# Position bias built behind the first feature-major chunk, and read back eight heads at a time

## The chip, the cores and the metric

The kernel runs on one core of one Trainium2 chip. Its engines are named as the profile names them: PE is TensorE (products, and PEld its weight loads), DVE is VectorE, ACT is ScalarE, POOL is GpSimd, SP is SyncE, whose queue issues the loads of weights. The metric is the device time of one execution in microseconds (us), as a median over runs.

## The reference

Two transformer blocks run one after the other on 256 tokens of width 1024, in float32. The change lies in the first block's mixer. It normalizes x, multiplies it by `w_in`, and runs two attentions on pieces of the product: `dsa_mixer` (8 heads, the 64 best keys of each query by an index score) and `nsa_mixer` (8 heads in 2 groups, three branches: compressed tokens, selected blocks, a window). All logits get a position bias that depends on the distance of query and key alone:

```python
bias = table_a[t5_bucket(dist)]                     # heads 0 to 7, dsa_mixer
bias_c = table_b[t5_bucket(t - cmp_end)]            # heads 8 to 15, compressed tokens
bias_s = tg[g_idx, t5_bucket(dist_s)]               # heads 8 to 15, selected blocks
bias_w = table_b[t5_bucket(dist_w)]                 # heads 8 to 15, window
...
blk = kv[:, idx] + pe[None, None, :, None, :]       # 15 overlapping blocks of 32 tokens
return jax.nn.gelu(blk @ w1) @ w2                   # compress_blocks, for k and for v
```

## The kernel before

Weights stream from HBM in units of 512 KB (two k-tiles of 512 columns). SP's queue loads a unit into `raw` (L246), ACT rounds it into `hi` (L262), DVE subtracts to get the remainder `lo` (L263), and PE multiplies the normalized, transposed x by both parts: a *streamed product* below is one such matmul (L349, L351, L352 where the output is feature-major, L305 to L307 where it is token-major). Units are loaded up to five ahead of their use and split up to two ahead.

The first block's projection is cut into nine chunks of columns, in the order 4, 0, 1, 3, 2, 5, 6, 7, 8 (48 streamed products for chunk 4, 72 for chunk 0, 96 for each of the others). Small work of other kinds is queued with `later` and put between the k-tiles of these chunks: the index scores and their top 64 (`index`, `topk`), the compression of keys and values (`cmp1`, `cmp1b`, `cmp2`), then the attention steps during chunks 5 to 8. On PE, DVE and ACT the order of instructions is a scheduler's, which follows the program's dependencies; on POOL and SP it is the order of the code, since `manual_schedule` is set for these two.

The position bias is made by `bias_job` (L588 to L602). A product of the one-hot buckets with the table `rel_bias` gives `tv`, 16 heads by 384 distances (L590, L592). It is written to DRAM sixteen times over (`tvd`, L595) and read back with a shifted start for each partition, in eight DMAs of 16 partitions and 256 KB each, so that `BT[p, h, j]` is the bias of query p and key j for head h (L597). Then `cmpB`, the bias of the compressed tokens with its mask, is set and filled by two copies out of BT (L600 to L602). `bias_job` is queued behind the top 64 and falls into chunk 3.

On POOL the following stands behind it in the code: memsets of `kcT` and `VB` (L741, L743), of `ge` for k and v in `cmp1b` (L773), and the gates (L988). Ahead of it stand the loads of the compression's weights `w1k`, `w1v` and small operands `csk`, `csv` (L703, L705), the copies of k and v into shifted pairs `kpk`, `kpv` (L717, L718) and the additions that make the blocks `blkk`, `blkv` (L725). Compression multiplies the blocks by `w1` (`cmp1`, L753), folds four partial sums (`cmp1b`, L763), applies the gelu on DVE and ACT into `ge` (L774) and multiplies by `w2` (`cmp2`, L783 for k, L790 for v). BT's readers are `cmpB`, the softmax of the branches (L866, heads 8 to 15) and `bm` on POOL (L842, heads 0 to 7 with the mask of the top 64). The branches come in the order selected, window, `dsa_mixer`, so that heads 0 to 7 are read last.

Of the kernel before, what the change touches and what calls it, by code (L numbers as in the profile page):

```python
# [23 lines left out]
NEG = -1.0e30  # L24
# [185 lines left out]
class Prog:  # L210
# [343 lines left out]
    def block1_mix(self, x0, x):  # L554
        tc, nc, ap, g = self.tc, self.nc, self.ap, self.g
        with ExitStack() as es, ExitStack() as rs_:
# [22 lines left out]
            tot = sum(CONSTS[n].shape[1] for n in C1)  # L579
            BT = cp.tile([128, 16, 256], F32, name="BT")  # L580
            cmpB = cp.tile([128, 2, 8, 16], F32, name="cmpB")
# [5 lines left out]

            def bias_job():  # L588
                ps = self.psm()
                nc.tensor.matmul(ps[:16, :384], rb, onehot, start=True, stop=True)  # L590
                tv = bp.tile([16, 384], F32, name="tv")
                nc.vector.tensor_tensor(tv, ps[:16, :384], neg, op=ALU.add)  # L592

                tvd = self.dp.tile([16, 16, 384], F32, name="tvd")
                nc.gpsimd.dma_start(tvd.rearrange("c h u -> h c u"), tv.unsqueeze(1).to_broadcast([16, 16, 384]))  # L595
                for i in range(8):
                    nc.gpsimd.dma_start(BT[16 * i:16 * i + 16, :, :],  # L597
                                        bass.AP(tensor=tvd.tensor, offset=tvd.offset + 127 - 16 * i,
                                                ap=[[16 * 384 - 1, 16], [384, 16], [1, 256]]))
                nc.gpsimd.memset(cmpB, NEG)  # L600
                nc.gpsimd.tensor_copy(cmpB[:, 1, :, 0:15], BT[:, 8:16, 31:256:16])
                nc.gpsimd.tensor_copy(cmpB[:, 0, :, 0:7], BT[:, 8:16, 159:256:16])  # L602

# [22 lines left out]
            def small_done(t, ps):  # L626
                nc.scalar.activation(tms[:, t, :], ps, AF.Copy, scale=r0[:, t:t + 1])
                if t:
                    nc.scalar.activation(gb, tms[:, :, 328:352], AF.Tanh, scale=0.5)
                    nc.gpsimd.tensor_scalar(gb, gb, 0.5, 0.5, op0=ALU.mult, op1=ALU.add)  # L630
                    nc.gpsimd.dma_start(caus, ap["c1"][:, tot - 256:])
                    nc.gpsimd.dma_start(rest, ap["c1"][0:32, 128:896])
                    nc.gpsimd.dma_start(rb, ap["rel_bias"])
            stats()
            self.gemm_tok(W_IN1, 4, *xT, small_done, acc=self.psm)
# [14 lines left out]
            self.later(rsB_job)  # L650
            self.gemm_feat(W_IN1, 0, *xT, d0)


# [47 lines left out]
            for nm in "kv":  # L701
                w1 = mp.tile([128, 16, 128], F32, name="w1" + nm)
                nc.gpsimd.dma_start(w1, ap["cmp_w1_" + nm])  # L703
                cs = mp.tile([128, 80], F32, name="cs" + nm)
                nc.gpsimd.dma_start(cs, ap["cmp_s_" + nm])  # L705
                cw.append((w1, cs))
            blks = []

            def d1(i, ps):
                nc.vector.tensor_tensor(kv[:, 2 * i:2 * i + 2, :], ps, bc2, op=ALU.mult)  # L710
                if i:
                    return
                for i, nm in enumerate("kv"):
# [6 lines left out]
                    blk = mp.tile([128, 16, 32], F32, name="blk" + nm)  # L720
                    nc.gpsimd.memset(blk[:, :, 30:32], 0.0)
                    for gr in range(2):
                        v = bass.AP(tensor=kp.tensor, offset=kp.offset + 256 * gr,
                                    ap=[list(kp.ap[0]), [2, 16], [16, 15]])
                        nc.gpsimd.tensor_tensor(blk[:, :, 15 * gr:15 * gr + 15], v,  # L725
                                                cw[i][1][:, 0:16].unsqueeze(2).to_broadcast([128, 16, 15]),
                                                op=ALU.add)
                    blks.append(blk)
            self.gemm_feat(W_IN1, 1, *xT, d1)

            def dq(q):
# [3 lines left out]
                return f  # L735
            self.later(bias_job)
            self.gemm_feat(W_IN1, 3, *xT, dq(qb))


            kcT = cp.tile([128, 2, 16], F32, name="kcT")  # L740
            nc.gpsimd.memset(kcT, 0.0)  # L741
            VB = cp.tile([128, 2, 4, 64], F32, name="VB")
            nc.gpsimd.memset(VB, 0.0)  # L743
            cps = {}
# [14 lines left out]
            def cmp1b(i):  # L759

                nm = "kv"[i]
                ps = self.psm()
                nc.tensor.matmul(ps[:, :32], cps[i], fold, start=True, stop=True)  # L763
                hx = mp.tile([128, 30], F32, name="hx" + nm)
                nc.vector.tensor_copy(hx, ps[:, :30])
                u = mp.tile([128, 30], F32, name="u" + nm)
                nc.vector.tensor_tensor(u, hx, hx, op=ALU.mult)
                nc.vector.tensor_scalar(u, u, 0.044715, 1.0, op0=ALU.mult, op1=ALU.add)
                nc.vector.tensor_tensor(u, u, hx, op=ALU.mult)
                th = mp.tile([128, 30], F32, name="th" + nm)  # L770
                nc.scalar.activation(th, u, AF.Tanh, scale=0.7978845608028654)
                ge = mp.tile([128, 2, 16], F32, name="ge" + nm)
                nc.gpsimd.memset(ge, 0.0)  # L773
# [50 lines left out]
            for br in (1, 2, 0):  # L824
                for t in (1, 0):
                    nh = 2 if t else 4
                    for u in range(4 // nh):
# [6 lines left out]
                        duos.append(duo)  # L834
            box = {}

            def bm(U):
# [3 lines left out]
                U["bm"] = bmp.tile([128, nh, n], F32, tag="bm", name="bm")  # L841
                nc.gpsimd.tensor_tensor(U["bm"], BT[:, h0:h0 + 2 * nh - 1:2, j0:j0 + n],  # L842
                                        M[:, t, :n].unsqueeze(1).to_broadcast([128, nh, n]), op=ALU.add)
# [15 lines left out]
            def softmax(U, ps):  # L859
# [4 lines left out]
                for i, h in enumerate(U["heads"]):  # L864
                    b = U["bm"][:, i, :] if br == 0 else BT[:, 8 + h, j0:j0 + n]
                    nc.vector.tensor_tensor_reduce(L[:, i, :], ps[:, i, :], b, op0=ALU.add, op1=ALU.max, scale=1.0,  # L866
# [769 lines left out]
```

## Time and profile before

| | |
|---|---|
| median of 3 runs | 1128.43 us (1125.5 to 1130.07) |
| profiled execution | 1129.25 us, of it span 1127.5 us |
| PE busy | 1104.7 us, 98% |
| DVE, ACT, POOL busy | 762.8, 573.7, 93.3 us |
| mean granted clock of PE | 0.993 |
| chain that ended last | PE 92%, DVE 3%, DMA 3%, of which BT<-tvd 2% of the span |

The profiled execution's time holds 1.75 us beside the span, which runs from the first to the last instruction. The chain that ended last is followed back from the end: 92% of it is work of PE. PE is busy in nearly all the span, so the places that matter are those at which it is not, and those at which its clock is lowered; both are found in time with the waits of PE and with windows.

### The profile page before, as it was taken

How to read it: one execution, taken by the hardware profiler on the slowest of the kernel's cores; microseconds unless marked ns; L12 is line 12 of the kernel's file. 1: busy time of each engine (PE TensorE's matmuls, PEld its weight loads, DVE VectorE, ACT ScalarE, POOL GpSimd, SP SyncE). 2: the span in 40 equal slices, each digit the busy share in tenths (PEclk: the TensorE clock that was granted, in tenths of full speed). 3: DMA queues.
4: the chain of work that ended last, by engine and by line, in shares of the span. 5: the costliest groups of instructions: out<-in, count | busy, mean ns of one | idle time of the engine just before them, and what ended most of it. 6: DMA issues, size and time to landing. Idle time of an engine off the chain costs nothing.

```text
span 1127.5 us, 17685 instructions
## 1 busy us (share of the span) xinstructions
PE 1104.7 (98%) x6852; PEld 986.4 (87%) x6852; DVE 762.8 (68%) x1230; ACT 573.7 (51%) x858; POOL 93.3 (8%) x135
## 2 busy tenths in 40 slices
PE   9998999999999999999999999999999999999997
PEld 8887899888888878888879999889999978888886
DVE  6766777677755567777458675556778777777643
ACT  6325544555544456555445336545555455655542
POOL 1411230000001010000001010001323000000000
PEclk9998999999999999999999999999999998999999
DMA  8794124655555646555556655444544565555552
GB/s 298 250 175 145 39 86 149 210 179 196 189 187 182 199 168 201 186 187 186 186 169 201 195 168 200 152 130 139 181 150 157 163 204 167 188 186 185 189 173 92
DMA packets 55908, 196.91 MB, mean 175 GB/s; under 512 B 6716, under 2 KB 6988, under 8 KB 55568
## 3 DMA queue, kind: packets, MB, share of 16 engines
q1 hardware_dynamic: 52704, 186.44, 50.2%
q0 software_dynamic: 2832, 9.21, 3.5%
q8 instruction: 54, 0.88, 0.3%
q14 instruction: 30, 0.25, 0.1%
q10 hardware_dynamic: 288, 0.14, 0.1%
HBM read 192.84 MB, written 1.44 MB: 172 GB/s over the span
## 4 chain that ended last, share of the span: by engine, by line
PE 92%; DVE 3%; DMA 3%; ACT 1%; issue 1%; POOL 0%; DVEq 0%; POOLq 0%; ACTq 0%
PE acc L368 20%; PE acc L369 10%; PE acc L305 10%; PE acc L306 9%; PE acc L307 9%; PE acc L351 8%; PE acc L349 8%; PE acc L352 8%; DMA BT<-tvd 2%; PE sm L854 2%; PE o L893 1%; DVE lo L263 1%; PE tr L880 1%; PE o L1437 1%; PE sm L1407 1%; PE tr L399 1%
## 5 line engine op out<-in xcount | busy, mean ns | idle before, releaser
L263 DVE TENSOR_TENSOR lo<-raw,hi 128x1024 fp32r<-128x1024 f32 (+2 forms) x356 | 433.3, 1219 | 264.8 <-ACT hi L262 262.4
L262 ACT ACTIVATE hi<-raw 128x1024 fp32r<-128x1024 f32 (+2 forms) x356 | 371.2, 1044 | 425.4 <-issue 120.9
L368 PE MATMUL acc<-xs,hi 128*128 128x512 f32 x960 | 340.4, 400 | 1.3 <-DVE sum L374 1.0
L369 PE MATMUL acc<-xs,lo 128*128 128x256 f32 x960 | 268.8, 281 | 0.0
L368 PEld LDWEIGHTS acc<-xs,hi 128*128 128x128 f32 x960 | 180.8, 189 | 44.8 <-DVE sum L374 1.4
L349 PE MATMUL acc<-xs,hi 128*128 128x256 f32 (+1 forms) x696 | 198.7, 288 | 0.3 <-ACT hi L262 0.3
L351 PE MATMUL acc<-xs,hi 128*128 128x256 f32 (+1 forms) x696 | 198.1, 286 | 0.0
L352 PE MATMUL acc<-xs,lo 128*128 128x256 f32 (+1 forms) x696 | 197.0, 286 | 0.1
L369 PEld LDWEIGHTS acc<-xs,lo 128*128 128x128 f32 x960 | 181.9, 189 | 0.5
L349 PEld LDWEIGHTS acc<-xs,hi 128*128 128x128 f32 (+1 forms) x696 | 132.9, 192 | 3.4 <-issue 2.4
L351 PEld LDWEIGHTS acc<-xs,hi 128*128 128x128 f32 (+1 forms) x696 | 133.5, 192 | 1.9 <-issue 1.5
L352 PEld LDWEIGHTS acc<-xs,lo 128*128 128x128 f32 (+1 forms) x696 | 132.8, 192 | 1.6 <-issue 1.0
L305 PE MATMUL acc<-hi,hT 128*128 128x512 f32 x304 | 117.9, 390 | 1.0 <-DVE x L1069 1.0
L306 PE MATMUL acc<-lo,hT 128*128 128x512 f32 x304 | 118.5, 390 | 0.0
L307 PE MATMUL acc<-hi,hT 128*128 128x512 f32 x304 | 118.0, 389 | 0.0
L305 PEld LDWEIGHTS acc<-hi,hT 128*128 128x128 f32 x304 | 57.1, 188 | 13.3 <-DVE x L1069 1.5
L307 PEld LDWEIGHTS acc<-hi,hT 128*128 128x128 f32 x304 | 57.1, 188 | 12.0
L306 PEld LDWEIGHTS acc<-lo,hT 128*128 128x128 f32 x304 | 57.1, 188 | 11.5
L305 PE MATMUL acc<-hi,xs 128*128 128x386 f32 (+1 forms) x128 | 47.7, 375 | 1.6 <-DVE f L1160 1.5
L306 PE MATMUL acc<-lo,xs 128*128 128x386 f32 (+1 forms) x128 | 48.0, 375 | 0.0
L307 PE MATMUL acc<-hi,xs 128*128 128x386 f32 (+1 forms) x128 | 46.8, 370 | 0.0
L374 DVE TENSOR_TENSOR sum<-acc,sum 128x512 f32<-128x512 f32 x60 | 41.0, 684 | 0.0
(430 smaller groups left out, 1344.5 us busy)
## 6 DMA issues: line engine op xcount, KB each, us to landing
raw<-in_w_in SPq DMA_DIRECT2D x100, 512.0 KB, 3.5
raw<-in_ffn_w_gate SPq DMA_DIRECT2D x44, 512.0 KB, 3.5
raw<-in_ffn_w_up SPq DMA_DIRECT2D x44, 512.0 KB, 3.4
raw<-in_ffn_w_down SPq DMA_DIRECT2D x44, 512.0 KB, 3.4
raw<-in_w_mlp_in SPq DMA_DIRECT2D x32, 512.0 KB, 3.4
raw<-in_w_mlp_out SPq DMA_DIRECT2D x32, 512.0 KB, 3.2
raw<-in_w_out SPq DMA_DIRECT2D x16, 512.0 KB, 3.5
raw<-in_w_in SPq DMA_DIRECT2D x16, 386.0 KB, 3.1
```

Of the source, the lines that this page charges most:

```text
L262: nc.scalar.activation(hi[:, :n * w], raw[:, :n * w], AF.Copy)
L263: nc.vector.tensor_tensor(lo[:, :n * w], raw[:, :n * w], hi[:, :n * w], op=ALU.subtract)
L305: nc.tensor.matmul(ps[t][:, :w], xh[:, k, sl], hi, start=(k == 0), stop=False)
L306: nc.tensor.matmul(ps[t][:, :w], xh[:, k, sl], lo, start=False, stop=False)
L307: self.last_mm = nc.tensor.matmul(ps[t][:, :w], xl[:, k, sl], hi, start=False, stop=last)
L349: nc.tensor.matmul(o, hi[:, fs], xh[:, k, :], start=(k == 0 and f % 2 == 0), stop=False, skip_group_check=True)
L351: nc.tensor.matmul(o, hi[:, fs], xl[:, k, :], start=False, stop=False, skip_group_check=True)
L352: nc.tensor.matmul(o, lo[:, fs], xh[:, k, :], start=False, stop=last, skip_group_check=True)
L368: nc.tensor.matmul(ps[:, f, :, :], hi[:, fs], x.both[:, k, :, :], start=(k == 0), stop=False)
L369: nc.tensor.matmul(ps[:, f, 0, :], lo[:, fs], x.hi[:, k, :], start=False, stop=last)
L374: nc.vector.tensor_tensor(s, ps[:, :, 0, :], s, op=ALU.add)
L854: nc.tensor.matmul(ps[:, i, :], q[pr:pr + 64, U["fts"][i], t * 128:t * 128 + 128], kk, start=True, stop=True)
```

## The change

The job is cut in two. `bias_table` makes `tv` and writes `tvd`; it is called right behind chunk 0 instead of being queued into chunk 3. `bias_rows(g)` reads back eight heads into a tile of their own: `BT[1]`, heads 8 to 15, ahead of chunk 1, and `BT[0]`, heads 0 to 7, behind the call of chunk 5. Each is eight DMAs of 16 partitions and 128 KB. The memsets of `kcT`, `VB`, `ge`, the tails of `blk` and `cmpB` are put ahead of the first read. The load of `w1k` and the small operands come behind that read, the copies kp of k and v come together, `w1v` behind them, then the additions and the two copies into `cmpB`. The operands `rest` and `rb` of the bias product are loaded ahead of the causal mask.

```diff
-            BT = cp.tile([128, 16, 256], F32, name="BT")
+            BT = [cp.tile([128, 8, 256], F32, name="BT%d" % g) for g in range(2)]
...
-            def bias_job():
+            box = {}
+
+            def bias_table():
+
                 ps = self.psm()
                 nc.tensor.matmul(ps[:16, :384], rb, onehot, start=True, stop=True)
                 tv = bp.tile([16, 384], F32, name="tv")
                 nc.vector.tensor_tensor(tv, ps[:16, :384], neg, op=ALU.add)
-
-                tvd = self.dp.tile([16, 16, 384], F32, name="tvd")
+                tvd = box["tvd"] = self.dp.tile([16, 16, 384], F32, name="tvd")
                 nc.gpsimd.dma_start(tvd.rearrange("c h u -> h c u"), tv.unsqueeze(1).to_broadcast([16, 16, 384]))
+
+            def bias_rows(g):
+
+                tvd = box["tvd"]
                 for i in range(8):
-                    nc.gpsimd.dma_start(BT[16 * i:16 * i + 16, :, :],
-                                        bass.AP(tensor=tvd.tensor, offset=tvd.offset + 127 - 16 * i,
-                                                ap=[[16 * 384 - 1, 16], [384, 16], [1, 256]]))
-                nc.gpsimd.memset(cmpB, NEG)
-                nc.gpsimd.tensor_copy(cmpB[:, 1, :, 0:15], BT[:, 8:16, 31:256:16])
-                nc.gpsimd.tensor_copy(cmpB[:, 0, :, 0:7], BT[:, 8:16, 159:256:16])
+                    nc.gpsimd.dma_start(BT[g][16 * i:16 * i + 16, :, :],
+                                        bass.AP(tensor=tvd.tensor, offset=tvd.offset + 8 * 384 * g + 127 - 16 * i,
+                                                ap=[[16 * 384 - 1, 16], [384, 8], [1, 256]]))
...
             self.gemm_feat(W_IN1, 0, *xT, d0)
+            bias_table()
...
             for nm in "kv":
-                w1 = mp.tile([128, 16, 128], F32, name="w1" + nm)
-                nc.gpsimd.dma_start(w1, ap["cmp_w1_" + nm])
-                cs = mp.tile([128, 80], F32, name="cs" + nm)
-                nc.gpsimd.dma_start(cs, ap["cmp_s_" + nm])
-                cw.append((w1, cs))
-            blks = []
+                cw.append((mp.tile([128, 16, 128], F32, name="w1" + nm), mp.tile([128, 80], F32, name="cs" + nm)))
+            blks = [mp.tile([128, 16, 32], F32, name="blk" + nm) for nm in "kv"]
+            kcT = cp.tile([128, 2, 16], F32, name="kcT")
+            VB = cp.tile([128, 2, 4, 64], F32, name="VB")
+            ges = [mp.tile([128, 2, 16], F32, name="ge" + nm) for nm in "kv"]
+            for tl in [kcT, VB] + ges + [b[:, :, 30:32] for b in blks]:
+                nc.gpsimd.memset(tl, 0.0)
+            nc.gpsimd.memset(cmpB, NEG)
+            bias_rows(1)
+            nc.gpsimd.dma_start(cw[0][0], ap["cmp_w1_k"])
+            for i, nm in enumerate("kv"):
+                nc.gpsimd.dma_start(cw[i][1], ap["cmp_s_" + nm])
...
+                    kps.append(kp)
+                nc.gpsimd.dma_start(cw[1][0], ap["cmp_w1_v"])
+                for i, kp in enumerate(kps):
                     for gr in range(2):
...
-                    blks.append(blk)
+                nc.gpsimd.tensor_copy(cmpB[:, 1, :, 0:15], BT[1][:, :, 31:256:16])
+                nc.gpsimd.tensor_copy(cmpB[:, 0, :, 0:7], BT[1][:, :, 159:256:16])
             self.gemm_feat(W_IN1, 1, *xT, d1)
...
-            self.later(bias_job)
             self.gemm_feat(W_IN1, 3, *xT, dq(qb))
...
             for c in range(4):
                 self.gemm_feat(W_IN1, 5 + c, *xT, gdone(c))
+                if c == 0:
+                    bias_rows(0)
```

What stands on POOL before, from the additions for v to the memset ahead of the gates (`Pc` is a tile of the attention on compressed tokens):

```order
L721 MEMSET blkv 128x16x2
L725 TENSOR_TENSOR blkv<-kpv,csv 128x16x15 x2
L595 DMA tvd<-tv 16x16x384
L597 DMA BT<-tvd 16x16x256 x8
L600 MEMSET cmpB 128x256
L601 COPY cmpB<-BT 128x8x15
L602 COPY cmpB<-BT 128x8x7
L741 MEMSET kcT 128x32
L743 MEMSET VB 128x512
L773 MEMSET gek 128x32
L773 MEMSET gev 128x32
L909 MEMSET Pc 128x512
```

And on POOL with the change, from the write of the table on (BT_175 is `BT[1]`; line numbers are those of the changed kernel):

```order
L597 DMA tvd<-tv 16x16x384
L703 COPY fold<-ident 32x32 x4
L712 MEMSET kcT 128x32
L712 MEMSET VB 128x512
L712 MEMSET gek 128x32
L712 MEMSET gev 128x32
L712 MEMSET blkk 128x16x2
L712 MEMSET blkv 128x16x2
L713 MEMSET cmpB 128x256
L603 DMA BT_175<-tvd 16x8x256 x8
L715 DMA w1k<-in_cmp_w_k 128x2048
L717 DMA csk<-in_cmp_s_k 128x80
```

The write of the table and half of its reads moved from behind the additions into blkv to a place ahead of compression's loads; the memsets moved from behind the copies into `cmpB` to a place ahead of the reads.

What follows on POOL with the change, with the semaphores that each instruction waits for. DMASW0 to DMASW7 are eight semaphores that POOL's DMAs take in turn, here from the eight reads of `BT[1]` on:

```order
L715 DMA w1k<-in_cmp_w_k 128x2048 [waits DMASW0_49]
L717 DMA csk<-in_cmp_s_k 128x80 [waits DMASW1_49]
L717 DMA csv<-in_cmp_s_v 128x80 [waits DMASW2_49]
L728 DMA kpk<-kv 64x256 [waits DMASW3_49]
L729 DMA kpk<-kv 64x255 [waits DMASW4_49]
L728 DMA kpk<-kv 64x256 [waits DMASW5_49]
L729 DMA kpk<-kv 64x255 [waits DMASW6_49]
L728 DMA kpv<-kv 64x256 [waits DMASW7_49]
L729 DMA kpv<-kv 64x255 [waits DMASW0_49]
L728 DMA kpv<-kv 64x256 [waits DMASW1_49]
L729 DMA kpv<-kv 64x255 [waits DMASW2_49]
L731 DMA w1v<-in_cmp_w_v 128x2048 [waits DMASW3_49]
```

Each of these is issued when the DMA eight before it has landed, so the copies and loads of compression moved into a chain behind the reads of `BT[1]`.

On PE before, the second product of compression stands behind 487 streamed products:

```order
L351 MATMUL acc<-xs,hi 128x256
L352 MATMUL acc<-xs,lo 128x256
L349 MATMUL acc<-xs,hi 128x256
L783 MATMUL sm<-gek,csk 64x16 x2
L790 MATMUL sm<-csv,gev 16x64 x8
L351 MATMUL acc<-xs,hi 128x256
```

With the change (L789 and L796 are the lines L783 and L790 of before) the one for k stands behind 448 and the one for v behind 458:

```order
L789 MATMUL sm<-gek,csk 64x16 x2
L351 MATMUL acc<-xs,hi 128x256
L352 MATMUL acc<-xs,lo 128x256
L349 MATMUL acc<-xs,hi 128x256
L351 MATMUL acc<-xs,hi 128x256
L352 MATMUL acc<-xs,lo 128x256
L349 MATMUL acc<-xs,hi 128x256
L351 MATMUL acc<-xs,hi 128x256
L352 MATMUL acc<-xs,lo 128x256
L349 MATMUL acc<-xs,hi 128x256
L351 MATMUL acc<-xs,hi 128x256
L796 MATMUL sm<-csv,gev 16x64 x8
```

Both moved ahead, 39 and 29 streamed products. Compression's first products moved back: for k from behind 318 streamed products to behind 390, for v from behind 351 to behind 399, and the bias product moved ahead, from behind 288 to behind 182. The first index product stands behind 177 before and behind 182, next to the bias product, with the change.

## Rows read from the trace of the kernel before

**Rows 1.** Page, busy time by engine

```profile
PE 1104.7 (98%) x6852; PEld 986.4 (87%) x6852; DVE 762.8 (68%) x1230; ACT 573.7 (51%) x858; POOL 93.3 (8%) x135
```

**Rows 2.** Waits of PE: us in total, times, longest

```profile
PE sm L783 <- DVE gek L774: 5.8, 1, 5.8
PE tr L399 <- DVE xs L403: 2.2, 2, 1.8
```

**Rows 3.** Timeline of PE: start, us, what [idle before <- releaser]

```profile
82.25 0.28 PE L349 MATMUL acc<-xs,hi 128*128 128x256 f32 x1
88.34 0.40 PE L783 MATMUL sm<-gek,csk 128*64 128x16 f32 x4 [5.82 <-DVE gek L774]
...
90.05 0.41 PE L351 MATMUL acc<-xs,hi 128*128 128x256 f32 x1
90.26 0.41 PE L352 MATMUL acc<-xs,lo 128*128 128x256 f32 x1
```

**Rows 4.** Timeline of DVE at the pause's end

```profile
88.10 0.19 DVE L774 SCALAR_TENSOR_TENSOR gek<-thk,hxk 128x30 f32<-128x30 f32 x1 [5.32 <-POOL gek L773]
```

**Rows 5.** Timeline of POOL, the reads and what is behind

```profile
62.37 4.48 POOL L597 DMA_DIRECT2D BT<-tvd  x8 [5.24 <-DMA tvd<-tv]
...
86.89 0.37 POOL L601 COPY cmpB<-BT 128x120 f32<-128x120 f32 x1 [19.72 <-DMA BT<-tvd]
...
87.94 0.12 POOL L773 MEMSET gek<- 128x32 f32 x1
```

**Rows 6.** Timeline of PE later, streamed products and another group

```profile
95.92 0.28 PE L349 MATMUL acc<-xs,hi 128*128 128x256 f32 x1
96.04 0.28 PE L351 MATMUL acc<-xs,hi 128*128 128x256 f32 x1
96.25 1.13 PE L854 MATMUL sm<-kv,qb 64*128 64x256 f32 x4
```

**Rows 7.** Windows: PE PEld DVE ACT POOL busy, PEclk, DMA share, GB/s

```profile
90.00:92.00 2.00, 2.00 (x14) 2.00 (x13) 0.83 (x2) 1.18 (x6) 0.00 (x0) 0.63 0.70 254
```

**Rows 8.** Timeline of ACT, rounding of a weight unit

```profile
85.68 1.06 ACT L262 ACTIVATE hi<-raw 128x1024 fp32r<-128x1024 f32 x1 [4.16 <-DMA raw<-in_w_in]
```

**Rows 9.** Timeline of PE, first index product, compression's w1v product

```profile
33.28 1.13 PE L664 MATMUL sm<-ki,qi 32*128 32x256 f32 x4
...
64.51 1.08 PE L753 MATMUL sm<-w1v,blkv 128*32 128x128 f32 x32
```

**Rows 10.** Chain that ended last, the bias product: start, us

```profile
54.90 0.76 PE sm L590 x2
```

**Rows 11.** Timeline of DVE, the bias addition

```profile
55.68 0.55 DVE L592 TENSOR_TENSOR tv<-sm,rest 16x384 f32<-16x384 f32 x1 [0.23 <-PE sm L590]
```

**Rows 12.** DMA issues to 130 us: KB each, median us to landing

```profile
w1v<-in_cmp_w_v POOLq DMA_DIRECT2D x1, 1024.0 KB, 8.9
tvd<-tv POOLq DMA_DIRECT2D x1, 384.0 KB, 5.6
...
kpv<-kv POOLq DMA_DIRECT2D x2, 64.0 KB, 2.5
```

**Rows 13.** DMA queues, 65 to 73: packets, MB, share of 16 engines

```profile
q0 software_dynamic: 318, 1.06, 101.6%
q1 hardware_dynamic: 20, 0.05, 4.2%
```

**Rows 14.** Tile BT, its DMAs

```profile
DMA to landing us min/median/max: 7.7/13.2/20.2
```

**Rows 15.** DMA queue of POOL, 35 to 41

```profile
q0 software_dynamic: 302, 2.09, 95.6%
```

**Rows 16.** Timeline of POOL, additions into blkk

```profile
45.61 1.67 POOL L725 TENSOR_TENSOR blkk<-kpk,csk 128x240 f32<-128x240 f32 x2 [7.49 <-DMA kpk<-kv]
```

**Rows 17.** Timeline of POOL, the first bm

```profile
129.90 2.51 POOL L842 TENSOR_TENSOR bm<-BT,M 128x512 f32<-128x512 f32 x2
```

**Rows 18.** Windows, columns as in rows 7

```profile
92.00:129.00 37.00, 37.00 (x258) 31.89 (x257) 26.18 (x92) 17.52 (x55) 3.66 (x4) 1.00 0.22 72
```

More of the change, by code (lines that the diff above doesn't have):

```diff
@@ L630, in small_done @@
                     nc.gpsimd.tensor_scalar(gb, gb, 0.5, 0.5, op0=ALU.mult, op1=ALU.add)
-                    nc.gpsimd.dma_start(caus, ap["c1"][:, tot - 256:])
                     nc.gpsimd.dma_start(rest, ap["c1"][0:32, 128:896])
                     nc.gpsimd.dma_start(rb, ap["rel_bias"])
+                    nc.gpsimd.dma_start(caus, ap["c1"][:, tot - 256:])
             stats()
@@ L712, in d1 @@
                     return
+                kps = []
                 for i, nm in enumerate("kv"):
@@ L718, in d1 @@
                         nc.gpsimd.dma_start(kp[64:128, gr, 0:255], src[:, 1:256])
-                    blk = mp.tile([128, 16, 32], F32, name="blk" + nm)
-                    nc.gpsimd.memset(blk[:, :, 30:32], 0.0)
+                    kps.append(kp)
+                nc.gpsimd.dma_start(cw[1][0], ap["cmp_w1_v"])
+                for i, kp in enumerate(kps):
                     for gr in range(2):
@@ L724, in d1 @@
                                     ap=[list(kp.ap[0]), [2, 16], [16, 15]])
-                        nc.gpsimd.tensor_tensor(blk[:, :, 15 * gr:15 * gr + 15], v,
+                        nc.gpsimd.tensor_tensor(blks[i][:, :, 15 * gr:15 * gr + 15], v,
                                                 cw[i][1][:, 0:16].unsqueeze(2).to_broadcast([128, 16, 15]),
                                                 op=ALU.add)
-                    blks.append(blk)
+                nc.gpsimd.tensor_copy(cmpB[:, 1, :, 0:15], BT[1][:, :, 31:256:16])
+                nc.gpsimd.tensor_copy(cmpB[:, 0, :, 0:7], BT[1][:, :, 159:256:16])
             self.gemm_feat(W_IN1, 1, *xT, d1)
@@ L735, in dq @@
                 return f
-            self.later(bias_job)
             self.gemm_feat(W_IN1, 3, *xT, dq(qb))
[L740 to L743, printed above, removed]
             cps = {}
@@ L771, in cmp1b @@
                 nc.scalar.activation(th, u, AF.Tanh, scale=0.7978845608028654)
-                ge = mp.tile([128, 2, 16], F32, name="ge" + nm)
-                nc.gpsimd.memset(ge, 0.0)
+                ge = ges[i]
                 nc.vector.scalar_tensor_tensor(ge[:, :, 0:15], th.rearrange("p (a b) -> p a b", a=2), 1.0,
@@ L834, in block1_mix @@
                         duos.append(duo)
-            box = {}
             def bm(U):
@@ L841, in bm @@
                 U["bm"] = bmp.tile([128, nh, n], F32, tag="bm", name="bm")
-                nc.gpsimd.tensor_tensor(U["bm"], BT[:, h0:h0 + 2 * nh - 1:2, j0:j0 + n],
+                nc.gpsimd.tensor_tensor(U["bm"], BT[0][:, h0:h0 + 2 * nh - 1:2, j0:j0 + n],
                                         M[:, t, :n].unsqueeze(1).to_broadcast([128, nh, n]), op=ALU.add)
@@ L864, in softmax @@
                 for i, h in enumerate(U["heads"]):
-                    b = U["bm"][:, i, :] if br == 0 else BT[:, 8 + h, j0:j0 + n]
+                    b = U["bm"][:, i, :] if br == 0 else BT[1][:, h, j0:j0 + n]
                     nc.vector.tensor_tensor_reduce(L[:, i, :], ps[:, i, :], b, op0=ALU.add, op1=ALU.max, scale=1.0,
```

## The prediction

> **What bounds the kernel now.** I read the busy table first: TensorE is busy for 98% of the span [rows 1], so only what TensorE executes, or what it stands still for, can move the time. Then the waits of TensorE: one line stands out, 5.8 us before the compression's second product (L783), which waits for `gek` from VectorE; the next longest is 2.2 us in total, much later [rows 2]. The timeline of TensorE shows that place: the last streamed product starts at 82.25, the next instruction at 88.34 [rows 3]. The chain behind it is read backwards. VectorE writes `gek` at 88.10 and had waited 5.32 us for GpSimd's memset of `gek` [rows 4]. That memset is a tenth of a microsecond of work, but it stands behind the two copies into `cmpB`, and those waited 19.72 us for the last of the eight reads of BT, issued from 62.37 on [rows 5]. So TensorE stands still because an unrelated memset is queued behind a 2 MB read. The stall has a second price: behind it the granted clock is at its lower level, 1.2 GHz. Products follow each other by 0.21 us at 90.05 [rows 3] against 0.12 at full clock [rows 6], and the mean granted clock of 0.63 over 90 to 92 [rows 7] puts the return to 2.4 GHz at about 91.5.
>
> **The change part by part.** The sum is made against the profiled execution, 1129.25 us, which is 0.8 us above the median of the three runs shown.
>
> *The memsets ahead of the reads.* `kcT`, `VB` and both `ge` are now set before any read of the table is issued. TensorE's 5.82 us [rows 3] go. What is late next? In the new order the second compression products come 39 and 29 streamed products earlier than before, so their own inputs must be there at about 77.5; see below. If instead the old order had merely lost its wait, TensorE would have run the compression's products and the 41 streamed products for which split weights were there, until at least 82.25 + 42 x 0.12 = 87.3; the following unit's rounding ends at 85.68 + 1.06 = 86.7 [rows 8], and its remainder follows on VectorE, so about then. So even with the whole read in the way weights would be late by little, and now half of the read is gone from that stretch. Minus 5.8.
>
> *The clock.* Without the pause nothing lowers it there: from 88.34 to 91.5 are 3.1 us at half speed, in which 1.55 us of work at full speed was done. Minus 1.5.
>
> *The table earlier.* The bias product on TensorE moves, it isn't added: the first qi.ki product stood behind 177 streamed products at 33.28 [rows 9], the bias product now stands behind 182, so at 33.9; 0.76 us of it [rows 10] and 0.55 us of VectorE's addition [rows 11] give 35.3. Its operands are loaded one place earlier than before. The write of the table lands 5.6 us after its issue [rows 12], at 40.9. GpSimd waits for it with everything else queued behind: the reads, `w1k`, the small loads and the copies kp. The four memsets and the fold copies stand ahead and are hidden in that wait.
>
> *The first half read.* In 65 to 73 the GpSimd queue alone kept all 16 engines busy (101.6%) and moved 1.06 MB [rows 13]: 0.98 us per half-size read, if engine time goes by bytes. The first whole read landed 7.7 us after its issue, the last 20.2 us [rows 14], which is 86.5. For halves that is a first landing at 40.9 + 7.7 - 1.0 = 47.6 and a last one at 54.5; the other bound is that a read takes as long as a whole one, 24.1 us from first issue to last landing, which gives 65. I take 55, nearest to the row with engine time. Weights starve meanwhile: in 65 to 73 their queue got 4.2% [rows 13]. TensorE did not feel that, since it waited for no weight until 82.25, and half the bytes starve it half as long.
>
> *Compression's loads behind it.* GpSimd's DMAs share eight semaphores, and each is issued only when the one eight before it has landed (the order with its waits shows it). So `w1k` follows the first landing, and its 1 MB follows the reads at the 2.09 MB in 6 us of [rows 15]: landed at 58. The second copy of kpv waits for that; three more issues bring 59.6, their landing 2.5 us more [rows 12]. The additions take 1.67 us a pair [rows 16]: blkk at 61.5, blkv at 63.7, the copies of `cmpB` at 64.5. `w1v` is issued at 59.7 and lands at 65, with the 8.9 us it took before [rows 12] at 68.6. When are they wanted? Before, the w1v product at 64.51 [rows 9] had 351 streamed products ahead; in the new order the w1k product has 390 ahead and the w1v product 399. 39 x 0.12 later, without the 1.1 us of the w1k product: 68.1; the second at 70.3. Margins: 6.6 us for blkk, 5.3 for `w1v`, 1.7 with the long load. No wait, so zero; both ends stay for the range.
>
> *The second half read* is issued behind the first two gate operations, some 88 us now, 4.5 us of issue on GpSimd. Landed by 103 with halves, by 112 with whole times. Its first reader, bm, ran at 129.90 [rows 17], so at about 122 now: nothing. From 92 to 129 the DMA engines were busy for 22% [rows 18], so the loads of weights have room beside it.
>
> *The order.* TensorE's list is newly interleaved: up to the 860th streamed product, 44 groups of other products stand between streamed ones instead of 48. Entering a group costs 0.21 us from start to start instead of 0.12 [rows 6]: 4 x 0.09 = 0.4, at most double if leaving costs as much, and nothing if the merged groups pay inside. Minus 0.4. VectorE's own order changes more, but from 92 to 129 it was busy for 26 of 37 us while TensorE was for all of it [rows 18].
>
> Sum: 1129.25 - 5.8 - 1.5 - 0.4 = 1121.5 on the profiled execution, 1120.7 against the median.
>
> One rule speaks against this. The Trainium skill, in "DMA: Bandwidth & Descriptors" under "Anatomy of one DMA", fits a GpSimd DMA as 2.0 us plus its bytes at 436 GB/s. By that a 128 KB read is an estimated 2.3 us against 2.6 for 256 KB, so halving would save an eighth and cutting eight reads into sixteen would nearly double their whole. By that fit the first half would end near the late bound of 65, the third rival. The trace disagrees so far: the engines were full over 8 us, with four reads' bytes moved, so the reads overlap and their data sets the pace.
>
> **The rivals.**
> 1. *A shorter wait takes the old one's place.* TensorE now meets several new meeting points (compression's first products, `gek` and `gev`, the logits against `cmpB`) on lists that the order has shifted against each other. For it: the margins above are 2 to 7 us and built from landing times that ranged from 2.5 to 20. Against it: TensorE showed no other wait of its own in block 1 even when the engines were full. A wait of 3 us without the clock's fall leaves 1120.7 + 3 = 1124.
> 2. *The gain is given back in attention.* If from 92 us on something other than TensorE set the pace, an earlier start would only wait longer there. For it: VectorE at 71% and its chain of softmax steps. Against it: no idle time of TensorE in that stretch. 1128.
> 3. *Slower: compression arrives late.* If the half reads take as long as whole ones, the last lands at 65, `w1k` at 68, and `w1v`, issued at 69.7, lands at 75 to 78.6, while TensorE wants it at 70.3: a wait of 5 to 8.3 us, with the clock's 1.5 again. 1120.7 + 9.8 = 1130.5. It decides from the point where `w1v` lands later than about 77. For it: each of these loads is chained by the semaphores to the reads. Against it: the engine time of [rows 13].
>
> **How the numbers follow.** Forecast 0.69, own range 1117 to 1123; rival 1 0.15; rival 2 0.07; rival 3 0.09. The measurement tells 0.5%, 5.6 us, from no change: below 1122.8 is faster. Of the forecast some 0.65 lies there, of rival 1 some 0.05: faster 0.70. Same: the rest of the forecast and of rival 1, rival 2, half of rival 3: 0.25. Slower 0.05, the runs of rival 3 in which more than `w1v` is late. The range goes from 1116 (5 us under the sum: the doubled switching term and the runs' own spread of some 4 us) to 1127, which leaves out most of rivals 2 and 3.
>
> **What would show it.** Right: no wait of TensorE over 1 us between 30 and 170; `gek` of VectorE before 77; full clock from 82 to 92; the BT reads' first half landed at 52 to 58; `w1v` landed before 70; the stretch behind the gates shifted as a whole by 7 to 8 us. Wrong: TensorE waiting at the w1k or w1v product; weights' rounding on ScalarE ending late enough that a streamed product waits; bm waiting for the second half; or the shift present at 100 us and gone at 170.

## The result, and the profile after

The changed kernel takes 1118.61 us (median of 4 runs, 1116.42 to 1120.01), the kernel before 1129.25 in the same comparison: ratio 0.9905, 95% interval 0.9883 to 0.9927, so 8 to 13 us faster. The forecast was 1120.7, range 1116 to 1127. The profiled execution of after takes 1120.01 us with a span of 1118.2. TensorE is as busy as in [rows 1], of a shorter span, and DMA's share of the chain that ended last is 0% instead of 3% (page, busy time and chain):

```profile
PE 1101.1 (98%) x6852; PEld 982.5 (88%) x6852; DVE 763.3 (68%) x1230; ACT 573.7 (51%) x858; POOL 98.2 (9%) x143
...
PE 95%; DVE 3%; ACT 1%; issue 1%; DMA 0%; DVEq 0%; ACTq 0%
```

The waits of TensorE (us in total, times, longest) have lost the line on `gek` of [rows 2]; what was second there leads now:

```profile
PE tr L399 <- DVE xs L403: 2.4, 2, 1.8
PE acc L305 <- DVE f L1166: 1.5, 1, 1.5
```

In the windows (columns as in [rows 7]) TensorE is busy all the time where it had stood still, and its granted clock is 1.00, the 2.4 GHz level, where [rows 7] had 0.63. The stretch of [rows 18] shows more instructions in the same 37 us (282 against 258), and a DMA share of 0.38 against 0.22, with the second half read now in it; no wait comes of it:

```profile
82.00:92.00 10.00, 10.00 (x65) 8.33 (x64) 8.46 (x28) 5.46 (x13) 2.86 (x4) 1.00 0.27 85
92.00:129.00 37.00, 37.00 (x282) 32.89 (x280) 27.06 (x92) 18.00 (x62) 11.80 (x14) 1.00 0.38 90
```

The timeline of GpSimd (start, us, what, idle before it and what ended that) carries the whole change and answers [rows 5]:

```profile
34.17 0.59 POOL L597 DMA_DIRECT2D tvd<-tv  x1 [2.72 <-DVE tv L595]
...
36.92 0.12 POOL L712 MEMSET gek<- 128x32 f32 x1
...
40.36 4.21 POOL L603 DMA_DIRECT2D BT<-tvd  x8 [2.89 <-DMA tvd<-tv]
...
53.24 0.52 POOL L728 DMA_DIRECT2D kpv<-kv  x1 [0.47 <-DMA BT<-tvd]
57.57 0.52 POOL L729 DMA_DIRECT2D kpv<-kv  x1 [3.81 <-DMA w1k<-in_cmp_w_k]
...
59.09 0.56 POOL L731 DMA_DIRECT2D w1v<-in_cmp_w_v  x1
59.72 1.64 POOL L736 TENSOR_TENSOR blkk<-kpk,csk 128x240 f32<-128x240 f32 x2
62.74 2.39 POOL L736 TENSOR_TENSOR blkv<-kpv,csv 128x240 f32<-128x240 f32 x2 [1.38 <-DMA kpv<-kv]
...
90.90 4.28 POOL L603 DMA_DIRECT2D BT<-tvd  x8
```

The memset of `gek` runs at 36.92 instead of 87.94. The first half read is issued at 40.36, and its last landing lets the next issue go shortly before 53.24; `w1k` has landed shortly before 57.57. The next rows give the landing times of the first half (33 to 60, tile BT), to be held against [rows 14], and that of `w1v` (DMA issues from 33 to 105: KB, median us to landing):

```profile
DMA to landing us min/median/max: 4.6/7.3/8.9
```

```profile
w1v<-in_cmp_w_v POOLq DMA_DIRECT2D x1, 1024.0 KB, 6.8
```

So `w1v` landed at 59.09 + 6.8 = 65.9. TensorE wanted the two weights here (its timeline):

```profile
66.41 1.08 PE L760 MATMUL sm<-w1k,blkk 128*32 128x128 f32 x32
68.69 1.08 PE L760 MATMUL sm<-w1v,blkv 128*32 128x128 f32 x32
```

No wait stands behind either row. The margin of `w1v` is 2.8 us.

Where the time went, I add up from the starts of all TensorE instructions between the 48th and the 860th streamed product (17 to 185 us in before, up to the first branch products), each from its start to the next one's, so that a wait counts to the instruction ahead of it. The columns: all; the streamed products; the logits of attention (`kv,qb` and `ka,qa`); the indexer's `ki,qi`; the rest.

```
                    all   streamed  logits  ki,qi   rest
before             167.1    110.5    17.3    6.8    32.6
p0_before_again    169.0    111.9    17.3    6.8    33.1
after              158.2    103.1    15.7    6.8    32.6
q0_after_again     158.2    103.1    15.7    6.8    32.6
e1_memsets_only    163.3    109.5    15.0    6.8    32.0
e2_memsets_back    158.2    103.1    15.7    6.8    32.6
e3_whole_early     164.0    103.7    19.4    6.8    34.0
e4_halves_only     160.3    104.1    17.5    6.8    32.0
p1_after_paired    151.5    103.3    10.1    6.8    31.4
p2_before_paired   157.7    108.9    10.1    6.8    32.0
p3_whole_paired    153.8    105.7     9.9    6.8    31.5
q1_index_paired    156.8    109.6    10.1    4.0    33.1
q2_loads_behind    148.4    102.3    10.1    4.0    31.9
```

(p0_before_again and q0_after_again are second profiles of the same two kernels.) After against before: 7.4 us of the 8.9 lie in the streamed products, and 1.5 in the logits. Of the 7.4, 5.8 are the wait. Some 1.0 is half clock: the ten steps from 89.24 to 91.52 in before, the first behind a group of other products, took 2.28 us, where 0.20 for the first and 0.12 for each other make 1.28. The last 0.6 is four crossings between streamed products and other groups that after has less. The same half clock took 0.3 us more from compression's second products (0.89 us against 0.58 in after), which other small groups of the rest give back. The forecast had nothing for the logits. They are seen in the groups by line too (busy us, mean ns, over 80 to 185), of before:

```profile
L854 PE MATMUL sm<-kv,qb 64*128 64x256 f32 (+1 forms) x64 | 13.5, 347 | 0.0
L854 PE MATMUL sm<-ka,qa 64*128 64x256 f32 (+1 forms) x32 | 5.0, 346 | 0.0
```

and of after:

```profile
L858 PE MATMUL sm<-kv,qb 64*128 64x256 f32 (+1 forms) x64 | 13.0, 348 | 0.0
L858 PE MATMUL sm<-ka,qa 64*128 64x256 f32 (+1 forms) x32 | 4.0, 356 | 0.0
```

The same 96 entries (the trace has two for each of these products), about as long each, keep TensorE busy for 17.0 instead of 18.5 us: more of them overlap. Both second profiles repeat the logits' time of their kernel, so it belongs to the build and not to the execution.

### The profile page after: what moved, and what is told of

Same layout as the page of the kernel before. It is cut to its first block, busy times and chain, and to the rows that moved or that the text cites. A ratio compares the mean times of both kernels' runs of the same rounds, so it can differ in the third digit from the quotient of the medians.

```text
span 1118.2 us, 17704 instructions
## 1 busy us (share of the span) xinstructions
PE 1101.1 (98%) x6852; PEld 982.5 (88%) x6852; DVE 763.3 (68%) x1230; ACT 573.7 (51%) x858; POOL 98.2 (9%) x143
## 4 chain that ended last, share of the span: by engine, by line
PE 95%; DVE 3%; ACT 1%; issue 1%; DMA 0%; DVEq 0%; ACTq 0%
PE acc L368 20%; PE acc L369 10%; PE acc L305 10%; PE acc L306 10%; PE acc L307 10%; PE acc L352 9%; PE acc L349 9%; PE acc L351 8%; PE o L897 1%; PE sm L858 1%; DVE lo L263 1%; PE tr L884 1%; PE o L1443 1%; PE sm L1413 1%; PE tr L399 1%; PE sm L668 1%
```

## Experiments: which part removes the wait

The first four kernels undo or do one part alone. Two theories: A, that the price was the place of the memset in GpSimd's order; B, that it was the late end of the read itself.

**The memsets alone**, in the kernel before:

```diff
+            ges = [mp.tile([128, 2, 16], F32, name="ge" + nm) for nm in "kv"]
+            for tl in [kcT, VB] + ges:
+                nc.gpsimd.memset(tl, 0.0)
             cw = []
...
-                nc.gpsimd.memset(ge, 0.0)
```

> The kernel before with one edit: kcT, VB and both ge are set to zero ahead of every read of the table; the whole 2 MB read stays where it was. Theory A, the memset queued behind the read is itself the price: the 5.8 us wait and 1.5 us of half clock go, 7 us faster than before, about 1122. Theory B, the price is the late end of the read, and the memset was only the first to show it: VectorE's addition of cmpB to the logits, in the new order behind 430 streamed products instead of 506, then stands still until the copies end at about 87, holds the roundings behind it, and TensorE waits 4 to 8 us there; within 3 us of before, 1126 to 1132.

Measured: 1124.82, ratio to before 0.9959 (0.9942 to 0.9976). The wait moves to the next reader of the table. Waits of TensorE:

```profile
PE sm L854 <- DVE Lc L918: 4.5, 1, 4.5
```

The timeline of VectorE shows why: the addition of `cmpB` to the logits stands for 5.28 us until GpSimd's copies are done, and TensorE goes on right behind it, as it did behind `gek` in [rows 3, 4]:

```profile
86.46 0.62 DVE L918 TENSOR_TENSOR Lc<-sm,cmpB 128x64 f32<-128x64 f32 x4 [5.28 <-POOL cmpB L602]
```

```profile
86.96 2.31 PE L854 MATMUL sm<-kv,qb 64*128 64x256 f32 x8 [4.52 <-DVE Lc L918]
```

Theory B holds, theory A falls. The time alone would not have said so: it lies between the two expectations. That this kernel is nevertheless 4 us faster than before is by the table above 1.3 of wait and 2.3 of logits, whose order came out differently.

**The memsets put back**, in the kernel after:

```diff
+            nc.gpsimd.memset(kcT, 0.0)
+            nc.gpsimd.memset(VB, 0.0)
             cps = {}
...
                 ge = ges[i]
+                nc.gpsimd.memset(ge, 0.0)
```

> The kernel after with one edit: the memsets of kcT, VB and both ge are put back behind the copies into cmpB on GpSimd, as before the change. TensorE's order is the same to within one streamed product. Theory B, the early half read is what counts: its reads landed at 52.96, GpSimd is through with the additions and the copies at about 67, and the first reader of a ge comes at about 76, so nothing waits: as after, within 1.5 us (1117 to 1120). Theory A, the place of the memsets is the price: TensorE waits for gek again, 4 us or more slower than after.

Measured: 1118.56, ratio to before 0.9913 (0.9894 to 0.9933), as after. The memset is done long before its reader, behind the copies of `cmpB` as it was before the change (timeline of GpSimd):

```profile
68.78 0.12 POOL L782 MEMSET gek<- 128x32 f32 x1
```

So with an early read the place of the memsets is worth nothing.

**The halves alone**, in the kernel before:

```diff
-            BT = cp.tile([128, 16, 256], F32, name="BT")
+            BT = [cp.tile([128, 8, 256], F32, name="BT%d" % g) for g in range(2)]
...
+                bias_rows(1)
...
                 self.gemm_feat(W_IN1, 5 + c, *xT, gdone(c))
+                if c == 0:
+                    bias_rows(0)
```

> The kernel before with one edit: the read is cut in two halves of eight heads, the first where the whole read was, the second behind the first gates; table, memsets and compression's loads stay where they were. The half read then lands at about 76 instead of 86.5, the memset of gek follows at about 77, and its reader stands behind 473 streamed products, at about 80. Theory B: wait and half clock go, 7.3 us faster than before; 51 groups instead of 49 give back 0.8 (at 0.39 each) or 0.2 (at 0.09 each): 1122 to 1123. Theory A, the early place is needed: a wait of 3 us or more stays, 1125 or more.

Measured: 1121.78, ratio 0.9941 (0.9922 to 0.996). GpSimd's timeline:

```profile
73.34 1.13 POOL L607 COPY cmpB<-BT 128x120 f32<-128x120 f32 x1 [7.60 <-DMA BT<-tvd]
...
75.15 0.12 POOL L779 MEMSET gek<- 128x32 f32 x1
```

With half the bytes the read ends at 73.3 instead of 86.9 [rows 5], in time for everything that stands behind it; TensorE has no wait there. This part alone gives 6.8 of the 8.9 us; the early place was not needed for the wait. What is missing is the logits' 1.8 us.

**The whole table read early**, in the kernel after:

```diff
             bias_rows(1)
+            bias_rows(0)
...
-                if c == 0:
-                    bias_rows(0)
```

> The kernel after with one edit: both halves of the table are read at the early place, 2 MB ahead of compression's loads; nothing is read behind the gates. The reads then land at about 61, w1k at 65, w1v at 74 to 76. TensorE's new order has compression's first products behind 466 and 468 streamed products (about 78) instead of 390 and 399. Theory B with a price of 0.39 us for each group of other products between streamed ones: 39 groups up to the 860th streamed product instead of 45, and no wait: 2.3 us faster than after, 1116. If groups cost 0.09 each: 0.5 us faster, 1118. Theory C, that cutting the read in two halves is itself needed (weights and w1v late behind 2 MB): a wait of 3 us or more at w1v or at a streamed product, 1121 to 1126.

Measured: 1124.96, ratio 0.9968 (0.9953 to 0.9982): 6 us slower than after. The figure is that of theory C, but the wait is not:

```profile
PE sm L761 <- DMA w1v<-in_cmp_w_v: 1.2, 1, 1.2
```

Most of the rest is in the logits (groups by line, 80 to 185), 20.9 us against 17.0 in after:

```profile
L859 PE MATMUL sm<-kv,qb 64*128 64x256 f32 (+1 forms) x64 | 14.4, 348 | 0.0
L859 PE MATMUL sm<-ka,qa 64*128 64x256 f32 (+1 forms) x32 | 6.5, 347 | 0.0
```

It has 39 groups of other products up to the 860th streamed product, the fewest of all, and the longest logits. A price per group cannot explain that. A small price there is: in the streamed column, which holds the crossings, the kernels without pause have 102.5 us with 39 groups (this one, without its 1.2 of wait), 103.1 with 45 (after) and 104.1 with 51 (e4_halves_only), about 0.13 us a group and not 0.39.

## Experiments: what the order of TensorE is worth

In [rows 6] a unit's logits begin with a row of four entries that takes 1.13 us. In after most such rows are alike, but some hold eight in the same time (timeline of TensorE):

```profile
82.81 1.13 PE L858 MATMUL sm<-kv,qb 64*128 64x256 f32 x4
...
127.93 1.13 PE L858 MATMUL sm<-ka,qa 64*128 64x256 f32 x8
```

A unit has two halves: keys on rows 0 to 63 and on rows 64 to 127 of the array, written to two PSUM tiles. Where the two halves stand alternately in TensorE's order they run beside each other; by their starts in the trace they follow each other by 0.01 us. Where the order has one half first and the other some products later, each pays in full; I take it that the second tile was still being read there. The Trainium skill, in "TensorE: Matmul & The Clock Gate" under "Why this matters for your kernels", says that products with few rows run concurrently when they lie in distinct row groups, and these rows agree (eight entries in the 1.13 us of four). In "TensorEngine Tiling (Array Packing)", "Gotcha 1: PSUM Pressure", it adds that different row tiles write to different PSUM banks; no run here tries one bank for both. The halves have a tile each, so a pair can be issued only when both tiles are free. Theory P: this is the order's share of the gain. Theory G: it is the number of groups, at 0.39 us each (some 1.55 us over four groups). The edit lets a unit's first product wait for the readers of both tiles, chains the others behind it, and puts them ahead of the products with V:

```diff
-                        nc.tensor.matmul(ps[:, i, :], q[pr:pr + 64, U["fts"][i], t * 128:t * 128 + 128], kk,
-                                         start=True, stop=True)
+                        with tc.issue_after(prev.ins) if prev else ExitStack():
+                            mm = nc.tensor.matmul(ps[:, i, :], q[pr:pr + 64, U["fts"][i], t * 128:t * 128 + 128], kk,
+                                                  start=True, stop=True)
+                        if not prev:
+                            for d in box.pop("reads", ()):
+                                tc.add_manual_dep(mm.ins, d.ins.name, mybir.DependencyInfo(
+                                    mybir.DependencyClass.Sync, mybir.DependencyReason.DATA), reason="both banks")
+                        prev = mm
...
+                box.setdefault("reads", []).append(d)
```

> The kernel after with one edit: the logits' products of a unit (two halves of 64 rows each, written to two PSUM tiles) are issued together, once both tiles have been read, and ahead of the products with V. Theory P, that the order's share of the gain is how many of these products run beside their other half: from the first logits to the 860th streamed product all 64 row pairs run two at a time; the time in logits falls from 15.7 us to 9 to 10, so 6 us faster than after, 1112 to 1114. Theory G, that the share is 0.39 us for each group of other products: 49 groups instead of 45 here, 1.6 us slower than after, 1120. A third way: the logits come later, the softmax chain sets the pace and TensorE waits 3 us or more before the branch products: as after or slower.

> The kernel before with the same edit as p1_after_paired. The 5.8 us wait for gek and the half clock behind it stay. Theory P: the time in logits falls from 17.25 us to 9 to 10, so 7.5 to 8 us faster than before, about 1121, and the distance to p1_after_paired is the wait and the clock alone, 7.3 us, not the 8.9 us between after and before up to the 860th streamed product. Theory G: 45 groups instead of 49: 1.6 us faster than before, 1127.

Measured: 1114.73 on after (ratio to before 0.9874, 0.9838 to 0.991), 1119.85 on before (0.9921, 0.9889 to 0.9954). Rows of eight throughout, and the logits' busy time falls to 10.7 us in both (p1_after_paired, timeline and groups by line):

```profile
91.64 1.14 PE L860 MATMUL sm<-kv,qb 64*128 64x256 f32 x8
```

```profile
L860 PE MATMUL sm<-kv,qb 64*128 64x256 f32 (+1 forms) x64 | 7.3, 346 | 0.0
L860 PE MATMUL sm<-ka,qa 64*128 64x256 f32 (+1 forms) x32 | 3.4, 343 | 0.0
```

Theory P holds and G falls: p1_after_paired has four groups more than after, and the table has it 6.7 us shorter, 5.6 of them in the logits. The edit also puts the products with V later; the other 1.1 us may be of that. (Its median is 3.9 us under that of after, a little above the 1112 to 1114 expected, and the two intervals overlap; the two profiled executions are 5.7 us apart, and the trace is the sharper witness.) With the logits equal, the table puts 6.2 us between p2_before_paired and p1_after_paired, 5.6 of them in the streamed products: the wait and the clock. That is under the 7.3 expected because the wait itself is shorter in that run:

```profile
PE sm L783 <- DVE gek L774: 4.3, 1, 4.3
```

**The whole read early, with the pairs:** e3_whole_early with the same edit.

> e3_whole_early (whole table read early) with the same edit. Theory P: what that kernel lost against after was the order (19.4 us in logits against 15.7) and 1.3 us of wait for w1v, so with the edit it is 1 to 2.5 us slower than p1_after_paired, 1114 to 1116, and reading the table in halves is worth little. Rival: the bigger read itself costs more than that wait (weights late, roundings late), and 4 us or more remain: 1117 or more.

Measured: 1112.73, a little under the expected, ratio 0.9872 (0.9839 to 0.9905), not to be told from p1_after_paired. Its trace still shows 1.5 us of wait at the w1v product:

```profile
PE sm L761 <- POOL Pc L922: 1.5, 1, 1.5
```

The row names the memset that came last on GpSimd; `w1v`, issued at 71.43, landed 8.7 us later, at 80.1, and the product starts at 80.23. So what the early whole read lost was the order. Reading in halves is worth 2.3 us by the table, 1.5 of them that wait, and nothing that the times can show, once the table is early and the logits are paired.

**Before, a second profile**, unchanged:

> The kernel before, unchanged, for a second profile. If the clock's rise at the start (full speed from 12.96 us in the first profile, from 9.97 in the profile of after) varies by chance, the 48th streamed product lies 0.7 to 1.4 us earlier than the 17.41 of the first profile, as in all five other traces; if it belongs to this build, it is at 17.4 again. The MLP's first products took 173 ns each in the first profile and 177 in four other builds: 173 again if that belongs to the build.

Measured: 1131.87, one run. The pause is there again, and the half clock behind it lasts longer: streamed products follow each other by 0.21 us until 92.93 instead of about 91.4. With 0.4 us more of pause that makes the 1.9 us by which the table has this profile above the first, so after gains 8.9 or 10.8 us over before, by which profile one takes (waits of TensorE and windows):

```profile
PE sm L783 <- DVE gek L774: 6.2, 1, 6.2
```

```profile
82.00:92.00 10.00, 4.18 (x35) 3.95 (x36) 3.15 (x5) 4.07 (x12) 1.69 (x7) 0.59 0.78 230
92.00:130.00 38.00, 38.00 (x259) 32.89 (x258) 25.79 (x93) 17.67 (x56) 3.98 (x4) 0.97 0.22 69
```

The 48th product is 0.95 us earlier than in the first profile, and the first part of the MLP (groups by line, 229 to 315) has the other of two durations. First of before, then of this second profile, then of after, then of after in a second profile:

```profile
L368 PE MATMUL acc<-xs,hi 128*128 128x512 f32 x242 | 84.1, 394 | 0.0
```

```profile
L368 PE MATMUL acc<-xs,hi 128*128 128x512 f32 x243 | 86.1, 399 | 0.0
```

```profile
L368 PE MATMUL acc<-xs,hi 128*128 128x512 f32 x213 | 75.3, 399 | 0.0
```

```profile
L368 PE MATMUL acc<-xs,hi 128*128 128x512 f32 x213 | 73.9, 394 | 0.0
```

Either build shows either duration, so that difference does not belong to the change. Nor does the start: the 48th product starts at 17.25 and 16.30 in before, at 15.80 and 15.98 in after, and at 17.51 in p3_whole_paired, which is built on after. Between the two first profiles they hide each other: 1.4 us to the good at the start, 1.5 us given back in the MLP.

**The indexer's products paired too**, on p1_after_paired, and after once more beside it:

```diff
-                        nc.tensor.matmul(ps[:, a, :n], qi[pr, a, t * 128:t * 128 + 128], ki[pr, :n], start=True,
-                                         stop=True)
+                        with tc.issue_after(prev.ins) if prev else ExitStack():
+                            mm = nc.tensor.matmul(ps[:, a, :n], qi[pr, a, t * 128:t * 128 + 128], ki[pr, :n], start=True,
+                                                  stop=True)
...
+                    box.setdefault("ireads", []).append(d)
```

> The kernel after, unchanged, for more times and a second profile beside q1_index_paired. About 1118.6 again, 0.9913 of before. The same parts of its accounting as in its first profile: 158.2 us from the 48th to the 860th streamed product, 15.7 us of them in logits.

> p1_after_paired with the same edit for the indexer's products too (32 rows each, two PSUM tiles): qi.ki is issued two at a time, once ScalarE has read both tiles. Theory P: their 6.8 us fall to 3.6 to 4, three of four groups lie in one piece: 3 us faster than p1_after_paired, about 1111. Theory G (0.39 us a group): 41 groups instead of 49 would give the same 3 us, so the time alone does not tell them apart here; the time of the 32 rows of qi.ki in the trace does. Rival: the mask comes later by the wait for both tiles, the top-k chain on VectorE is late, TensorE waits: no gain.

Measured: after again 1120.2 (0.991, 0.9886 to 0.9935), with the same 158.2 and 15.7 us; q1_index_paired 1117.73 (0.9892, 0.9865 to 0.992). The pairs came (groups by line, 28 to 80; after, then this kernel):

```profile
L668 PE MATMUL sm<-ki,qi 32*128 32x256 f32 (+1 forms) x32 | 7.3, 348 | 0.0
```

```profile
L670 PE MATMUL sm<-ki,qi 32*128 32x256 f32 (+1 forms) x32 | 4.4, 351 | 0.0
```

but TensorE, now ahead of its loads, waits at compression's products, and the granted clock falls in that stretch (waits of TensorE, then the window 60 to 78):

```profile
PE sm L768 <- DMA w1v<-in_cmp_w_v: 2.9, 1, 2.9
PE sm L868 <- DVE nm L885: 1.1, 1, 1.1
PE sm L768 <- POOL blkk L744: 1.0, 1, 1.0
```

```profile
60.00:78.00 18.00, 14.08 (x140) 13.12 (x139) 11.93 (x38) 3.80 (x5) 7.33 (x11) 0.81 0.57 201
```

The expected time was 6.7 us too low. The danger named there, a late mask, did not come: the mask was done by 78, and its first reader ran at 123. The 1.1 us (L868) are a unit of logits that waits until VectorE has read both tiles. The larger danger was `w1v`, the load with the 2.8 us margin. The remedy follows from GpSimd's timeline of after: kpv's second copy waits 3.81 us for `w1k`, and `w1v` stands behind it.

```diff
-            nc.gpsimd.dma_start(cw[0][0], ap["cmp_w1_k"])
...
-                nc.gpsimd.dma_start(cw[1][0], ap["cmp_w1_v"])
+                for i, nm in enumerate("kv"):
+                    nc.gpsimd.dma_start(cw[i][0], ap["cmp_w1_" + nm])
```

> q1_index_paired with one edit: w1k and w1v are loaded on GpSimd behind the small loads and the copies kp instead of w1k ahead of them. In q1_index_paired w1v landed at 69.99 and TensorE, ahead by 3 us, waited 2.9 us for it, and 1.0 us for blkk, because the last copies of kpv are issued only when w1k has landed. Here no copy stands behind a 1 MB load: copies landed by 56 to 58, w1k by 60, w1v by 64; the products stand behind 414 and 426 streamed products, at about 66 and 69. Then no wait, no half clock, and the 2.7 us of the indexer's pairs stay: 1110 to 1112. If weights of the stream are late instead (2 MB ahead of them in the queues), TensorE waits for a rounding on ScalarE and the gain is smaller: 1114 or more.

Measured: 1108.59, a little under the expected, ratio to before 0.9811 (0.9779 to 0.9843), 10 us faster than after and the fastest of all. In its trace TensorE has no wait over 1 us between 30 and 185.

## Why the prediction was right, and where it was not

- **The wait and the clock** (minus 5.8 and 1.5) are the bulk of the gain, as forecast: 5.8 and, in the first profile of before, 1.3 us (1.0 in streamed products, 0.3 in compression's).
- **What caused the wait** was told too narrowly. The prediction blamed an unrelated memset behind the read, and reckoned that without it TensorE would run on until 87.3. e1_memsets_only does just that and still stands for 4.5 us, because the logits with `cmpB` need the same read; and putting the memsets back costs nothing (e2_memsets_back). The term came out right by the other part of the change, the early half read, not by the move that the prediction credited with it. The change works because the read ends before its first reader; half the bytes suffice for that (e4_halves_only), and so does the early place, up to the 1.2 and 1.5 us at `w1v` (e3_whole_early, p3_whole_paired).
- **The landing times** held: the write of the table at 34.17 + 5.6 = 39.8 (40.9 forecast), the half read's last landing at about 53 (55), `w1k` at 57 (58), blkk at 61.4 (61.5), blkv at 65.1 (63.7), `w1v` at 65.9 (65). The second half was issued at 90.9 and landed by 102; its first reader, bm, ran at 117.
- **The margins** were smaller than forecast: 5.0 us for blkk and 2.8 for `w1v` instead of 6.6 and 5.3, because TensorE came 1.7 us earlier than reckoned, most of it the start that varies from run to run, and `w1v` landed 0.9 later. It was enough; q1_index_paired shows how near rival 1 was.
- **The order** (minus 0.4) is the term that failed. What it priced, the crossing of groups, was right: entering takes 0.21 us and leaving 0.20 instead of 0.12, and four groups fewer gave some 0.6. What it left out is how many logits run two at a time, another 1.5 us. Together they are over its upper bound, the double. That the new order came out with more pairs was luck: nothing in the change aims at it, and in other builds the logits came out 2.1 us above before (e3_whole_early) and 2.3 below (e1_memsets_only).
- **Rival 2** did not occur: the lead of 10.4 us over the first profile at the 692nd streamed product, in the midst of attention's last units, is still 10.4 at the first product of the MLP (223.48 against 213.12). **Rival 3** rested on half reads taking as long as whole ones. Eight reads of 128 KB took 12.6 us from first issue to last landing, eight of 256 KB 24.1. The Trainium skill's fit in "DMA: Bandwidth & Descriptors", "Anatomy of one DMA", gives an estimated 2.6 and 2.3 us for one DMA of either size; added up over eight, as the prediction did, these would be nearly alike, and the trace disagrees.

The time itself came out 2.1 us under the forecast's 1120.7. Against before in the same comparison the drop is 10.6 us (8 to 13) where 7.7 were forecast. On the profiled execution the table's 8.9 us (5.8 of wait, 1.3 of clock, 0.6 of crossings, 1.5 of logits, less 0.3 in the rest) in place of 7.7 make the sum 1120.3, and it took 1120.01. That this is so close is luck too: the start and the MLP, which vary from run to run, happened to cancel.

## What to carry to other kernels

When an engine waits for something small that is queued behind a big transfer, look for the next reader of that transfer before blaming the queue: moving the small thing alone moves the wait. When a scheduler writes a new order, compare how long the same instructions keep the engine busy, not how many groups there are: products on separate rows of the array that lose their neighbour cost double. And before speeding up the engine ahead of a load, note the load's margin; a gain larger than the margin turns into a wait and a clock at half speed.

## What the runs showed of the hardware

Products on different rows of the array start 0.01 us apart, and eight entries take the 1.13 us of four; with 64 rows the 96 entries of the logits fall from 17.0 to 10.7 us, with 32 rows the indexer's from 7.3 to 4.4. The products of the MLP's first part run at 394 or at 399 ns in different runs of the same build, a difference of 1.5 us over that part, and the 48th product starts 0.95 us apart in two runs of before and 1.7 us apart at most over all traces. The half clock behind one and the same pause ended at about 91.4 in one run and after 92.9 in another; no row shows a reason for any of these.
